# Hybrid GLA and SSD layer: the first head's k loaded and split in the start, half of q and k placed behind the last adaLN sums

## The chip, the cores and the metric

The kernel runs on one core of a Trainium2 chip. The metric is the device time of one execution in microseconds (us). Five engines work side by side, each on its own list of instructions in a fixed order: PE (matrix multiply), DVE (vector), ACT (scalar and copy), POOL (a second, slower vector engine) and SP (here it only issues DMAs).

## What is computed

One layer over 512 latent tokens and 256 context tokens of width 1024. A vector c gives six modulation parts (adaLN); the normed input, scaled and shifted by them, goes through one wide input projection, whose columns feed a gated linear attention branch (GLA, 4 heads, two directions) and a Mamba-2 branch (SSD, 4 groups, two directions). Both are merged under gates, projected and added; a SwiGLU feed-forward and a final norm follow. In short:

```python
ada = silu(c) @ w_ada + b_ada                  # sh1, sc1, g1, sh2, sc2, g2
h   = rms_norm(x, norm1_w) * (1 + sc1) + sh1   # latent; context with its own ada
q, k, v, r, lr_f, lr_b, z, xs, B, C, dt, ga, gb = split(h @ w_in)
g   = log_sigmoid(lr @ up + bias) / 16         # GLA gates of one direction
o_a = gla(q, k, v, g) both ways;  y_a = (rms_norm(o_a) * silu(r)) @ w_pa
o_b = ssd(xs, B, C, dt) both ways; y_b = rms_norm((o_b + d * xs) * silu(z)) @ w_pb
x   = x + g1 * ((sigmoid(ga) * y_a + sigmoid(gb) * y_b) @ w_out)
x   = x + g2 * swiglu(rms_norm(x, norm2_w) * (1 + sc2) + sh2)
out = rms_norm(x, final_norm_w)
```

## The kernel before, in words

Every matrix product is made in three passes, since its operands are split into a hi half of short mantissa and a lo half that holds the rest: hi x hH, hi x hL, lo x hH. A weight block of 512 KB is loaded by `load_raw` (L173, DMA on SP's queue, L176) into one of three buffers of the tag `raw`; `split_w` (L183) then makes hi by a copy on ACT (L188) and lo by a subtraction on DVE or, in some stages, POOL (L189). `load_w` (L194) gives both halves one of two buffers each (tags `whi`, `wlo`).

The start loads x, normalizes and transposes it (`xnT`), and makes the first adaLN parts in four batches: `ada_first` runs sixteen passes on PE over a batch of w_ada (L277, tile `ada`), copies the sum on ACT (`ar`, L280), turns it on PE (`adaT`, L283) and adds the bias on DVE (L288, then the scale `s`, L291). Each batch gives two of the eight k tiles of the modulated input: `h_of` makes hH on ACT (L299), the full value on DVE (L300) and hL on DVE (L301). The weights `misc` (the low-rank gate inputs and dt) and q of head 0 are loaded and split ahead in this block (the dictionary `ahead`).

`proj_cols` (L349) projects one block over the eight k tiles: `l_...` holds 512 latent columns (L361, L362, L366), `c_...` 256 context columns (L364, L365, L368), each in a PSUM bank of its own. `proj_rows` (L372) makes products by rows of tokens, `r_...`, for v, r and z (L386 to L388), its weights in two halves. Later adaLN columns are made one by one in `some_ada` (L329): every second call loads 512 KB (`raw_ada`) and sums it on POOL (L341, L343, L345), and a pass on PE finishes the one before (L336); the calls are spread over the projections, four of them in each v and r.

From misc's product come the GLA gates: copies into `M` (L396 to L398), their halves `MS` (L413 to L415), the matrix `U` (L407, L408), `pre` on PE (L470), three ACT functions and one DVE step (L472 to L475), then a write to memory, `gdr` (L476). The first GLA chain reads it back as `g` (L514) and makes sums with it on PE (`gc`, `kx`, `ky`, L501), which open the states `S`. At the end of the layer's first half the merge of both branches (`tgm`, `mt`, L967 to L978) runs beside the last block of w_pb and the start of w_out, which is scaled by g1 on POOL (L187); the scale of the second norm is made on DVE (`sc`, L952) with `n` (L950).

The order of the instructions on each engine is set by a scheduler that works on the whole program; `tc.high_priority()` and `tc.issue_after(instruction)` change the rank of what is written inside them.

## Time and profile before

| | us |
|---|---|
| median of 3 runs | 1431.89 (1430.45 to 1432.89) |
| profiled execution | 1434.66 |
| its span in the trace | 1432.9 |
| PE busy | 1357.3 (95%) |
| DVE busy | 871.0 (61%) |
| ACT busy | 502.2 (35%) |
| POOL busy | 465.4 (32%) |

The mean granted clock of TensorE in that execution is 0.981 of full speed. The profile's times count from the start of the span. A busy share is a mean over stages with different limits, so a stage is read from its own stretch of time: which engine stood still there, and what ended its wait.

### The profile page before, as it was taken

The numbers are of one execution on the slowest core, as the hardware profiler recorded it, in microseconds if no ns is written. First come the engines' busy times: TensorE is split into PE (matmuls) and PEld (weight loads), VectorE is DVE, ScalarE is ACT, GpSimd is POOL, SyncE is SP. The second block draws the span as 40 slices with busy tenths as digits, with TensorE's granted clock in tenths as the row PEclk, the third lists the DMA queues.
The fourth block names the chain that finished last, engine by engine and source line by source line (L and its number), as shares of the span: only waits on it lengthen the run. The fifth ranks groups of instructions, "written<-read, shape, count | busy, mean of one in ns | idle before, by whom it ended". The sixth has DMA issues, their size and how long they took to land.

```text
span 1432.9 us, 19032 instructions
## 1 busy us (share of the span) xinstructions
PE 1357.3 (95%) x7462; PEld 1152.4 (80%) x7462; DVE 871.0 (61%) x1292; ACT 502.2 (35%) x828; POOL 465.4 (32%) x333
## 2 busy tenths in 40 slices
PE   5999999999999999999899899999789999999997
PEld 3798999899888778877877787877578888888886
DVE  4559676563785787569758866766883343433225
ACT  6464333433444223433322342322243222222222
POOL 1355554245234433543253334113651122100001
PEclk9899999999999999999899999999999999999999
DMA  9363323334231343232322332557423333333331
GB/s 367 124 211 108 95 92 112 102 104 144 70 96 60 125 126 96 74 109 83 96 70 84 98 110 78 173 168 253 147 87 101 120 118 116 120 117 91 101 103 73
DMA packets 58010, 169.19 MB, mean 118 GB/s; under 512 B 6064, under 2 KB 10304, under 8 KB 57792
## 3 DMA queue, kind: packets, MB, share of 16 engines
q1 hardware_dynamic: 55328, 157.96, 34.0%
q0 software_dynamic: 2304, 9.64, 2.1%
q8 instruction: 59, 0.97, 0.3%
q10 hardware_dynamic: 288, 0.36, 0.1%
q14 instruction: 31, 0.25, 0.1%
HBM read 156.23 MB, written 11.72 MB: 117 GB/s over the span
## 4 chain that ended last, share of the span: by engine, by line
PE 66%; DVE 15%; DMA 9%; issue 6%; ACT 2%; POOL 2%; SPq 1%; POOLq 0%; DVEq 0%; ACTq 0%
DMA E<-cdr 5%; PE up L1056 3%; PE gate L1055 3%; PE gate L1056 3%; PE up L1055 3%; PE gate L1054 3%; PE up L1054 3%; PE db L204 3%; PE db L206 3%; PE db L205 3%; DVE E L747 2%; PE lv L501 2%; PE r_z L386 1%; PE pb_pb L632 1%; PE pb_pb L634 1%
## 5 line engine op out<-in xcount | busy, mean ns | idle before, releaser
L341 POOL TENSOR_TENSOR raw_ada<-raw_ada,cs 128x1024 f32<-128x1024 f32 x32 | 63.7, 1990 | 279.5 <-DMA raw_ada<-in_wts_dram 227.9
L747 DVE TENSOR_TENSOR E<-E,ebias 128x512 f32<-128x512 f32 x64 | 54.7, 859 | 49.4 <-DMA E<-cdr 49.3
L386 PE MATMUL r_z<-whi_z,hH 128*128 128x256 f32 x256 | 75.7, 298 | 6.6 <-DVE z L698 6.6
L343 POOL TENSOR_TENSOR raw_ada<-raw_ada 128x512 f32<-128x512 f32 x64 | 80.0, 1250 | 4.3
L388 PE MATMUL r_z<-whi_z,hL 128*128 128x256 f32 x256 | 76.9, 301 | 0.0
L387 PE MATMUL r_z<-wlo_z,hH 128*128 128x256 f32 x256 | 74.7, 293 | 0.0
L1054 PE MATMUL gate<-h2H,whi_gate 128*128 128x512 f32 (+1 forms) x192 | 71.8, 374 | 0.0
L1055 PE MATMUL gate<-h2L,whi_gate 128*128 128x512 f32 (+1 forms) x192 | 71.7, 373 | 0.0
L1056 PE MATMUL gate<-h2H,wlo_gate 128*128 128x512 f32 (+1 forms) x192 | 71.5, 373 | 0.0
L189 POOL TENSOR_TENSOR wlo_xs<-raw_xs,whi_xs 128x1024 fp32r<-128x1024 f32 x16 | 43.1, 2693 | 63.8 <-ACT whi_xs L188 63.8
L1056 PE MATMUL up<-h2H,wlo_up 128*128 128x512 f32 x160 | 63.0, 394 | 0.0
L1055 PE MATMUL up<-h2L,whi_up 128*128 128x512 f32 x160 | 62.3, 389 | 0.0
L1054 PE MATMUL up<-h2H,whi_up 128*128 128x512 f32 x160 | 62.2, 389 | 0.0
L189 DVE TENSOR_TENSOR wlo_gate<-raw_gate,whi_gate 128x1024 fp32r<-128x1024 f32 x20 | 33.2, 1661 | 45.2 <-ACT whi_gate L188 45.2
L189 DVE TENSOR_TENSOR wlo_down<-raw_down,whi_down 128x1024 fp32r<-128x1024 f32 x18 | 22.0, 1225 | 62.4 <-ACT whi_down L188 62.3
L386 PEld LDWEIGHTS r_z<-whi_z,hH 128*128 128x128 f32 x256 | 50.9, 200 | 9.2 <-DVE z L698 7.3
L170 POOL TENSOR_TENSOR rr_f<-rv_f,negh 128x1 f32<-128x1 f32 x4 | 2.6, 662 | 168.5 <-DVE rv_f L168 168.5
L189 POOL TENSOR_TENSOR wlo_z<-raw_z,whi_z 128x1024 fp32r<-128x1024 f32 x16 | 39.4, 2462 | 53.5 <-ACT whi_z L188 51.4
L386 PE MATMUL r_v<-whi_v,hH 128*128 128x256 f32 x192 | 55.7, 290 | 1.0 <-ACT whi_v L188 1.0
L205 PE MATMUL db<-wlo_down,fH 128*128 128x512 f32 x142 | 55.2, 389 | 0.0
L206 PE MATMUL db<-whi_down,fL 128*128 128x512 f32 x142 | 55.2, 389 | 0.0
L388 PE MATMUL r_v<-whi_v,hL 128*128 128x256 f32 x192 | 55.1, 287 | 0.0
(475 smaller groups left out, 4460.1 us busy)
## 6 DMA issues: line engine op xcount, KB each, us to landing
raw_ada<-in_wts_dram SPq DMA_DIRECT2D x32, 512.0 KB, 3.6
E<-cdr SPq DMA_DIRECT2D x64, 256.0 KB, 3.4
raw_gate<-in_wts_dram SPq DMA_DIRECT2D x22, 512.0 KB, 3.6
raw_up<-in_wts_dram SPq DMA_DIRECT2D x22, 512.0 KB, 3.5
raw_down<-in_wts_dram SPq DMA_DIRECT2D x22, 512.0 KB, 3.5
aw<-in_wts_dram SPq DMA_DIRECT2D x8, 1024.0 KB, 15.4
raw_xs<-in_wts_dram SPq DMA_DIRECT2D x16, 512.0 KB, 3.6
raw_z<-in_wts_dram SPq DMA_DIRECT2D x16, 512.0 KB, 3.7
```

The costliest lines, as they stand in the source:

```text
L189: (nc.gpsimd if split_pool[0] else nc.vector).tensor_tensor(lo, raw, hi.bitcast(F32), ALU.subtract)
L205: nc.tensor.matmul(out_, aH, bL, start=False, stop=False)
L206: nc.tensor.matmul(out_, aL, bH, start=False, stop=stop)
L341: nc.gpsimd.tensor_tensor(raw, raw, cs[:, :, 0:1].to_broadcast([P, KD, P]), ALU.mult)
L343: nc.gpsimd.tensor_tensor(raw[:, 0:n, :], raw[:, 0:n, :], raw[:, n:2 * n, :], ALU.add)
L386: nc.tensor.matmul(o, hH[:, kk, tk], hi[:, k, :], start=st, stop=False, skip_group_check=True)
L387: nc.tensor.matmul(o, hH[:, kk, tk], lo[:, k, :], start=False, stop=False, skip_group_check=True)
L388: nc.tensor.matmul(o, hL[:, kk, tk], hi[:, k, :], start=False, stop=sp, skip_group_check=True)
L747: nc.vector.tensor_tensor(ed, ed, ebias[:, d, n, hh].unsqueeze(2).to_broadcast([P, EH, P]), ALU.add)
L1054: nc.tensor.matmul(pts[kj][:, tk], hi[:, k, :], h2H[:, k, tk], start=(k == 0), stop=False)
L1055: nc.tensor.matmul(pts[kj][:, tk], hi[:, k, :], h2L[:, k, tk], start=False, stop=False)
L1056: nc.tensor.matmul(pts[kj][:, tk], lo[:, k, :], h2H[:, k, tk], start=False, stop=(k == KD - 1))
```

## The change

k of head 0 is loaded and split in the start block, right behind misc and q. Its halves, `k_hi` and `k_lo`, do not take the buffers of `whi` and `wlo` but two of the three `raw` buffers; they are created only when k's raw tile exists. The context product of k, c_k, takes the second half of the bank that holds c_misc, without a start flag of its own and ranked behind misc's first context matmul. The last four k tiles of q and of k in head 0 are ranked behind the last adaT matmul. The matmuls of the context products skip a check of the compiler on accumulation groups. v of head 0 no longer calls `some_ada`; the columns that it loaded move on to the calls behind it.

```diff
--- before.py
+++ after.py
@@ -183,6 +183,8 @@
     def split_w(key, hi, lo, row=None):
         with nullcontext() if in_start[0] else tc.high_priority():
             raw = load_raw(key)
+            if callable(hi):
+                hi, lo = hi(), lo()
             if row is not None:
                 nc.gpsimd.tensor_tensor(raw[:, 0, :], raw[:, 0, :], row, ALU.mult)
             nc.scalar.activation(hi, raw, AF.Copy)
@@ -267,7 +269,11 @@
         in_start[0] = True
         for key in (("misc",), ("q", 0)):
             ahead[key] = load_w(key)
+
+        ahead[("k", 0)] = split_w(("k", 0), *[lambda n=n: wp.tile([P, KD, P], F32R, tag="raw", name=f"k_{n}", bufs=3) for n in ("hi", "lo")])
         in_start[0] = False
+
+        ada_end = [None]
 
         def ada_first(b):
             pt = sm_bank(f"ada_{b}")
@@ -280,7 +286,7 @@
                 nc.scalar.activation(ar, pt, AF.Copy)
                 pt = sm_bank(f"adaT_{b}")
                 for j in range(4):
-                    nc.tensor.matmul(pt[:, 2 * j:2 * j + 2], ar[:, j * P:(j + 1) * P], sel, start=True, stop=True)
+                    ada_end[0] = nc.tensor.matmul(pt[:, 2 * j:2 * j + 2], ar[:, j * P:(j + 1) * P], sel, start=True, stop=True)
                 pv = pt[:, 0:8].rearrange("p (c j t) -> p c j t", c=2, t=2)
                 k0 = 2 * b
                 for c in range(2):
@@ -345,6 +351,8 @@
             nc.gpsimd.tensor_tensor(pr_, raw[:, 0, :], raw[:, 1, :], ALU.add)
             half_done.append((j, pr_))
 
+    early_cx, misc_start = [], []
+
 
     def proj_cols(key, with_ctx):
         if key[0] in ("q", "k") and key[1:2] != (0,):
@@ -355,17 +363,33 @@
         hi, lo = load_w(key)
         nm = "_".join(map(str, key))
         lat = mm_bank("l_" + nm)
-        cx = mm_bank("c_" + nm) if with_ctx else None
-        for k in range(KD):
-            st, sp = k == 0, k == KD - 1
-            nc.tensor.matmul(lat, hi[:, k, :], hH[:, k, 0:SEQ], start=st, stop=False)
-            nc.tensor.matmul(lat, hi[:, k, :], hL[:, k, 0:SEQ], start=False, stop=False)
-            if with_ctx:
-                nc.tensor.matmul(cx[:, 0:CTX], hi[:, k, :], hH[:, k, SEQ:NT], start=st, stop=False)
-                nc.tensor.matmul(cx[:, 0:CTX], hi[:, k, :], hL[:, k, SEQ:NT], start=False, stop=False)
-            nc.tensor.matmul(lat, lo[:, k, :], hH[:, k, 0:SEQ], start=False, stop=sp)
-            if with_ctx:
-                nc.tensor.matmul(cx[:, 0:CTX], lo[:, k, :], hH[:, k, SEQ:NT], start=False, stop=sp)
+
+        joined = key == ("k", 0)
+        if joined:
+            cx = early_cx[0][:, CTX:2 * CTX]
+        else:
+            cx = mm_bank("c_" + nm) if with_ctx else None
+        if key == ("misc",):
+            early_cx.append(cx)
+        first = key in (("q", 0), ("k", 0))
+        with ExitStack() as late_part:
+            for k in range(KD):
+                st, sp = k == 0, k == KD - 1
+                if joined and k == 0:
+                    late_part.enter_context(tc.issue_after(misc_start[0].ins))
+                if first and k == 4:
+                    late_part.enter_context(tc.issue_after(ada_end[0].ins))
+                nc.tensor.matmul(lat, hi[:, k, :], hH[:, k, 0:SEQ], start=st, stop=False)
+                nc.tensor.matmul(lat, hi[:, k, :], hL[:, k, 0:SEQ], start=False, stop=False)
+                if with_ctx:
+                    m_ = nc.tensor.matmul(cx[:, 0:CTX], hi[:, k, :], hH[:, k, SEQ:NT], start=st and not joined, stop=False,
+                                          skip_group_check=True)
+                    if key == ("misc",) and k == 0:
+                        misc_start.append(m_)
+                    nc.tensor.matmul(cx[:, 0:CTX], hi[:, k, :], hL[:, k, SEQ:NT], start=False, stop=False, skip_group_check=True)
+                nc.tensor.matmul(lat, lo[:, k, :], hH[:, k, 0:SEQ], start=False, stop=sp)
+                if with_ctx:
+                    nc.tensor.matmul(cx[:, 0:CTX], lo[:, k, :], hH[:, k, SEQ:NT], start=False, stop=sp, skip_group_check=True)
         return lat, cx
 
 
@@ -373,7 +397,7 @@
         banks = [mm_bank(f"r_{'_'.join(map(str, keyf(0)))}_{b}") for b in range(ntile // 2)]
         for kh in range(2):
             hi, lo = load_w(keyf(kh))
-            if keyf(0)[0] in "vr":
+            if keyf(0)[0] in "vr" and keyf(0)[:2] != ("v", 0):
                 some_ada()
                 some_ada()
             for i in range(ntile):
```

What the scheduler makes of it shows in the order of the instructions. First PE around the fourth adaT (`adaT`, fed by `sel` and `ar`), before and then changed:

```order
L361 MATMUL l_q_583<-hH,whi_q_149 128x512
L362 MATMUL l_q_583<-hL,whi_q_149 128x512
L366 MATMUL l_q_583<-hH,wlo_q_150 128x512
L283 MATMUL adaT_373<-sel,ar_371 128x2 x4
L361 MATMUL l_misc<-hH,whi_misc 128x512
L361 MATMUL l_q_583<-hH,whi_q_149 128x512
L364 MATMUL c_misc<-hH,whi_misc 128x256
L362 MATMUL l_misc<-hL,whi_misc 128x512
L365 MATMUL c_misc<-hL,whi_misc 128x256
L366 MATMUL l_misc<-hH,wlo_misc 128x512
L368 MATMUL c_misc<-hH,wlo_misc 128x256
L361 MATMUL l_misc<-hH,whi_misc 128x512
```

```order
L382 MATMUL l_k_617<-hH,k_hi 128x512
L383 MATMUL l_k_617<-hL,k_hi 128x512
L390 MATMUL l_k_617<-hH,k_lo 128x512
L289 MATMUL adaT_379<-sel,ar_377 128x2 x4
L382 MATMUL l_q_589<-hH,whi_q_149 128x512
L383 MATMUL l_q_589<-hL,whi_q_149 128x512
L390 MATMUL l_q_589<-hH,wlo_q_150 128x512
L382 MATMUL l_q_589<-hH,whi_q_149 128x512
L383 MATMUL l_q_589<-hL,whi_q_149 128x512
L390 MATMUL l_q_589<-hH,wlo_q_150 128x512
L382 MATMUL l_k_617<-hH,k_hi 128x512
L383 MATMUL l_k_617<-hL,k_hi 128x512
```

Before, six tiles of q stand ahead of adaT and misc directly behind it; now it is four tiles of q and four of k, and behind adaT come two more of each before misc. The first r_v follows 36 rows behind adaT, and c_k (named c_misc<-hH,k_hi) 31 rows of r_v later.

Second, DVE from misc's copies to the products of the gates, before and then changed:

```order
L396 COPY M<-l_misc 16x512
L396 COPY M<-c_misc 16x256
L189 TENSOR_TENSOR wlo_k_612<-raw_k_613,whi_k_611 128x1024
L413 CAST MS_462<-M 32x768
L408 TENSOR_TENSOR U<-early_in,U 32x1024
L415 TENSOR_TENSOR MS_462<-M,MS_462 32x768
L189 TENSOR_TENSOR wlo_v_0_683<-raw_v_0_684,whi_v_0_682 128x1024
L398 COPY M<-l_misc 64x512
L398 COPY M<-c_misc 64x256
L413 CAST MS_466<-M 32x768
L415 TENSOR_TENSOR MS_466<-M,MS_466 32x768
```

```order
L420 COPY M<-l_misc 16x512
L420 COPY M<-c_misc 16x256
L191 TENSOR_TENSOR wlo_v_0_682<-raw_v_0_683,whi_v_0_681 128x1024
L437 CAST MS_468<-M 32x768
L422 COPY M<-l_misc 64x512
L422 COPY M<-c_misc 64x256
L437 CAST MS_472<-M 32x768
L439 TENSOR_TENSOR MS_468<-M,MS_468 32x768
L439 TENSOR_TENSOR MS_472<-M,MS_472 32x768
L432 TENSOR_TENSOR U<-early_in,U 32x1024
L191 TENSOR_TENSOR wlo_v_1_760<-raw_v_1_761,whi_v_1_759 128x1024
L461 COPY kv_616<-c_misc 128x256
```

Before, k's lo half stands behind the first copies, and v's first between the two MS products; now v's first half stands where k's was, all copies come ahead of the MS products, U goes last, and the copy of c_k (kv<-c_misc) follows v's second half.

Third, PE where the second direction of head 0's gates is first read (`gc_1`), before and then changed:

```order
L361 MATMUL l_q_1301<-hH,whi_q_1295 128x512
L362 MATMUL l_q_1301<-hL,whi_q_1295 128x512
L366 MATMUL l_q_1301<-hH,wlo_q_1296 128x512
L501 MATMUL gc_1_1021<-mkr,g_1_1019 128x128 x2
L501 MATMUL kx_1_1028<-g_1_1019,mkr 128x384
L501 MATMUL gc_1_1021<-mkr,g_1_1019 128x128
L501 MATMUL ky_1_1030<-g_1_1019,mkr 128x256
L501 MATMUL gc_1_1021<-mkr,g_1_1019 128x128
L501 MATMUL ky_1_1030<-g_1_1019,mkr 128x128
L501 MATMUL S_0_0_1051<-kv_610,kd_0_1014 128x256 x2
L361 MATMUL l_q_1301<-hH,whi_q_1295 128x512
```

```order
L390 MATMUL l_q_1280<-hH,wlo_q_1275 128x512
L342 MATMUL ada_1308<-one,apr_1272 128x1
L382 MATMUL l_k_1324<-hH,whi_k_1318 128x512
L383 MATMUL l_k_1324<-hL,whi_k_1318 128x512
L390 MATMUL l_k_1324<-hH,wlo_k_1319 128x512
L382 MATMUL l_k_1324<-hH,whi_k_1318 128x512
L383 MATMUL l_k_1324<-hL,whi_k_1318 128x512
L390 MATMUL l_k_1324<-hH,wlo_k_1319 128x512
L385 MATMUL c_k_1325<-hH,whi_k_1318 128x256
L389 MATMUL c_k_1325<-hL,whi_k_1318 128x256
L525 MATMUL gc_1_1000<-mkr,g_1_998 128x128 x2
L525 MATMUL kx_1_1007<-g_1_998,mkr 128x384
```

Before, nine matmuls of head 1's q stand ahead of gc_1 and 15 behind S_0_0; now all 24 stand ahead of it, with six of head 1's k and two of its context product.

## Rows read from the trace of the kernel before

**Rows 1.** The page: busy time and share of the span, instructions by engine.
```profile
PE 1357.3 (95%) x7462; PEld 1152.4 (80%) x7462; DVE 871.0 (61%) x1292; ACT 502.2 (35%) x828; POOL 465.4 (32%) x333
```

**Rows 2.** Stretches: from:to, length, busy (count) per engine, PEclk, DMA share, GB/s.
```profile
51.00:54.30 3.30, 0.92 (x4) 0.53 (x4) 2.35 (x7) 2.50 (x4) 0.00 (x0) 1.00 0.00 0
54.30:57.70 3.40, 3.40 (x10) 2.83 (x11) 2.34 (x4) 0.00 (x0) 1.05 (x2) 0.50 0.02 5
57.70:61.00 3.30, 2.38 (x11) 1.38 (x10) 2.54 (x4) 1.28 (x2) 0.65 (x2) 1.00 0.80 202
109.60:116.00 6.40, 6.35 (x20) 5.20 (x21) 5.61 (x9) 5.67 (x8) 5.49 (x5) 0.52 0.28 90
116.00:150.00 34.00, 32.74 (x224) 29.98 (x222) 33.09 (x54) 13.68 (x23) 18.05 (x13) 1.00 0.27 90
```

**Rows 3.** PE in order of time: start, us, line, operation, out<-in, count [idle <-releaser].
```profile
41.35 0.40 PE L361 MATMUL l_q<-hH,whi_q 128*128 128x512 f32 x1
...
42.49 1.06 PE L277 MATMUL ada<-aw,csw 128*32 128x512 f32 x8
...
50.01 0.95 PE L283 MATMUL adaT<-sel,ar 128*128 128x2 f32 x8
52.32 0.50 PE L361 MATMUL l_misc<-hH,whi_misc 128*128 128x512 f32 x1 [1.37 <-ACT hH L299]
...
54.26 0.79 PE L362 MATMUL l_misc<-hL,whi_misc 128*128 128x512 f32 x1 [1.06 <-DVE hL L301]
...
58.26 0.28 PE L368 MATMUL c_misc<-hH,wlo_misc 128*128 128x256 f32 x1
...
59.39 0.50 PE L361 MATMUL l_k<-hH,whi_k 128*128 128x512 f32 x1 [0.39 <-ACT whi_k L188]
...
60.65 0.50 PE L366 MATMUL l_k<-hH,wlo_k 128*128 128x512 f32 x1 [0.53 <-DVE wlo_k L189]
...
65.77 0.28 PE L364 MATMUL c_k<-hH,whi_k 128*128 128x256 f32 x1
...
66.60 1.09 PE L470 MATMUL pre<-U,MS 96*128 96x512 f32 x4
...
69.57 0.28 PE L386 MATMUL r_v<-whi_v,hH 128*128 128x256 f32 x1
```

**Rows 4.** ACT in order of time, 30 to 73 us.
```profile
37.01 2.51 ACT L299 ACTIVATE hH<-xnT,ada,s 128x512 fp32r<-128x512 f32 x4 [2.62 <-DVE s L291]
...
58.27 1.06 ACT L188 ACTIVATE whi_k<-raw_k 128x1024 fp32r<-128x1024 f32 x1 [4.32 <-issue]
...
67.03 2.07 ACT L472 ACTIVATE ge<-pre 128x512 f32<-128x512 f32 x4 [0.24 <-PE pre L470]
```

**Rows 5.** DVE in order of time, 30 to 76 us.
```profile
51.00 0.23 DVE L288 TENSOR_TENSOR ada<-adaT,vecs 128x4 f32<-128x4 f32 x2 [9.46 <-PE adaT L283]
...
59.39 1.20 DVE L189 TENSOR_TENSOR wlo_k<-raw_k,whi_k 128x1024 fp32r<-128x1024 f32 x1
...
66.68 0.42 DVE L398 COPY M<-c_misc 64x256 f32<-64x256 f32 x1
```

**Rows 6.** PE in order of time, 105 to 117 us.
```profile
109.65 1.19 PE L501 MATMUL gc<-mkr,g 128*128 128x128 f32 x4 [2.83 <-DMA g<-gdr]
...
115.40 0.75 PE L361 MATMUL l_q<-hH,whi_q 128*128 128x512 f32 x1
```

**Rows 7.** The page: costliest groups, the two POOL lines of an adaLN sum.
```profile
L341 POOL TENSOR_TENSOR raw_ada<-raw_ada,cs 128x1024 f32<-128x1024 f32 x32 | 63.7, 1990 | 279.5 <-DMA raw_ada<-in_wts_dram 227.9
...
L343 POOL TENSOR_TENSOR raw_ada<-raw_ada 128x512 f32<-128x512 f32 x64 | 80.0, 1250 | 4.3
```

**Rows 8.** Stretch from 845 to 895 us, columns as in rows 2.
```profile
845.00:895.00 50.00, 50.00 (x256) 40.88 (x256) 30.59 (x48) 17.23 (x29) 20.90 (x12) 0.95 0.26 85
```

**Rows 9.** DVE in order of time, around the merge: scale of the second norm.
```profile
993.02 2.40 DVE L952 SCALAR_TENSOR_TENSOR sc<-sc,n 128x512 f32<-128x512 f32 x1 [2.61 <-DMA n<-in_rows_dram]
```

**Rows 10.** PE's waits from 970 to 1062 us: total, times, longest.
```profile
PE ob L205 <- DVE wlo_out L189: 5.9, 3, 3.0
```

## The prediction

> **What bounds the kernel now.** First the page's busy times: PE works 1357.3 of 1432.9 us, 95% [rows 1]. The change takes no matmul away, so it can only shorten stretches in which PE stands still or runs at the lower clock. Next the table by stretch, for the place that the change touches [rows 2]: from 51.0 to 54.3 us PE is busy 0.92 of 3.30; from 54.3 to 57.7 it is busy all the time, but with a granted clock of 0.50, which is the 1.2 GHz level; from 57.7 to 61.0 it is busy 2.38 of 3.30. That is 2.38 + 0.92 us of idleness and 1.70 us (half of 3.40) of lower clock: 5.0 us lost in ten. Then PE's own instructions say why [rows 3]. The fourth adaT runs at 50.01, and the rest of misc waits for what follows from it: 1.37 us for hH, 1.06 us for hL. Behind misc come q's last two tiles, and then k waits 0.39 us for the hi and 0.53 us for the lo half of its weights. PE has nothing else to do: of q six tiles were already used up ahead of adaT, and k's split on ACT starts only at 58.27 [rows 4]. On DVE the 9.46 us ahead of 51.00 are idle time that ends with the same adaT [rows 5].
>
> **The change, part by part.** *k split early.* Two more instructions enter the start: k_hi on ACT, 1.06 us by whi_k's row, in an idle stretch of 2.62 us ahead of the third hH batch [rows 4]; and k_lo on DVE, 1.20 us by wlo_k's row [rows 5], ahead of the third batch's ada and s, which come 1.2 us later. That batch is needed by the misc tiles after 41 us, and DVE has 9.46 us free behind it, so I cost both at nothing; without that cover it would be 1.2 us. The same two instructions leave the place at 58.27 and 59.39. k's load itself is no new DMA: it is third among the weights on SP in both kernels.
>
> *The list on PE.* I count what lies between the first l_q at 41.35 and the first r_v at 69.57 [rows 3]. 22 matmuls of 512 columns fill 60.65 to 65.77, 0.233 each; 24 of 256 columns and four pre of 512 fill 65.77 to 69.57, which leaves 0.12 for one of 256. The list is 24 l_q, 24 l_k and 12 l_misc (60 x 0.233 = 14.0), 12 c_misc and 24 c_k (36 x 0.12 = 4.3), sixteen ada passes (2 x 1.06), adaT (0.95) and four pre (0.93): 22.3 us. The stretch took 28.22, so 5.9 us went into waits, the lower clock and the starts behind waits, 5.0 of them as read above. In the new order four tiles of q and four of k run ahead of adaT, and twelve matmuls of 0.233, 2.8 us, behind it. The first hL that PE now needs comes 3.3 us after adaT's end (54.26 against 50.96); ahead of it stand those 2.8 us and 0.8 us of hH matmuls, so the latency is covered by 0.3 us. Without c_k and pre, which now stand behind v's first matmuls, r_v could start at 41.35 + 22.3 - 2.9 - 0.9 = 59.8. What is late next: v. Its hi half takes misc's buffer, so it can start only when misc's last hi pass is through; after that PE has five matmuls, some 1.2 us, and the split needs 1.06 on ACT and then 1.20 on DVE behind the first copies into M. By the same kind of wait at k (0.39 + 0.53 = 0.92) I take 1.1 us for v, bounds 0.5 and 2.3, and 0.4 us (0 to 1) where pre now stands, ahead of which the c_k pass is done and little is left to hide M, MS and U. So this stretch gives 5.9 - 1.5 = 4.4 us.
>
> *The gates.* Their first matmul stood 8.34 us behind misc's last (66.60 against 58.26) [rows 3]. Five matmuls (1.05 us) ahead of r_v's 59.8 misc ends at about 58.8 now, 0.5 later; one split instead of two lies inside that chain (-1.2), but U has gone last in it (its own length is bounded by the splits', 0 to 1.2), and ACT makes v's second hi half (1.06) ahead of the first gate instead of behind it. I take the gates 1.4 us later, bounds 0 and 3. This is what counts next: at 109.65 PE stands 2.83 us for g of the second direction [rows 6], which comes out of those gates, and the wait costs a second time: from 109.6 to 116.0 the granted clock is 0.52. Before, 15 l_q came behind that block (from 115.40 on); now they stand ahead of it, with 6 l_k and 2 c_k: 21 x 0.233 + 2 x 0.12 = 5.1 us. PE comes 4.4 us earlier and does 5.1 us more, so it arrives about 0.7 us later than it did and still waits. With g later by 1.4 us, equal work is done 5.1 - 1.4 = 3.7 us earlier: the term is -0.7 against the stretch ahead of it. Head 1's k stands ahead of the gates' last two writes on SP, so its weights need not be late for this.
>
> *The adaLN sums.* Two loads of 512 KB and their sums leave v of head 0; each later pair slides up, and two come to lie in the gate and SSD stage near 845 to 895 us. A sum is 1.99 us and twice 1.25 us on POOL [rows 7] and one small addition: about 4.5, 9 for both. POOL is busy 20.90 of those 50 us, and PE waits for nothing there: 50.00 of 50.00 [rows 8]. Cost taken: 0.
>
> *The merge.* With other instructions in other places the order near 970 to 1015 us changes too: DVE's scale of the second norm, which waits 2.61 us for n [rows 9] and stood behind the last block's weights, goes ahead of two of them; the loads of g1 and of that norm go ahead of the four hres loads. Upwards I bound this with that 2.61, downwards with half of the 5.9 us that PE waits for the output weights [rows 10], since they come through g1. Nothing in the trace says which is nearer; I take 0.
>
> **Sum.** -4.4 + 0.7 + 0 + 0 = -3.7 us. The profiled execution took 1434.66 us and would take 1431.0. The median of the runs shown is 2.77 us below that execution, so I forecast **1428.2 us**.
>
> **Rivals.** *The second direction's gates set the end* (13%). DVE is busy 33.09 of the 34.0 us from 116 to 150 [rows 2], and it works on what g brings. If this chain, not PE's list, ends that stretch, all that was won waits there, and the gates' delay of 0 to 1.4 us shows: 1431.9 to 1433.3. For it: PE and DVE are both near full (32.74 against 33.09). Against it: PE's matmuls of head 1 can fill.
>
> *c_k waits for the copies of M* (5%). c_k now writes the second half of the bank that holds c_misc, and c_misc's last copy into M ended at 67.10 [rows 5]. By the list r_v starts at 59.8 + 1.1, and c_k stands 31 of its matmuls (3.7 us) behind, at 64.6. If the copies kept their time, PE would stand 2.5 us there: -3.7 + 2.5 = -1.2, 1430.7 us. Against it: in the new order the copies stand ahead of the products MS that came first before. The Trainium skill speaks for the wait: PSUM — Partial Sum Buffer, section PSUM bank collisions raise a hardware error, says that two engines must not use one bank on the same partitions at once and that access is to be guarded by bank, whichever columns are meant; no row of this trace shows it, since each product had a bank of its own.
>
> *The merge gives back its 2.61 us* (5%): -1.1, 1430.8.
>
> *The change doesn't do what it says* (3%): the new cover behind adaT is too short or v's weights take over k's wait in full, the lower clock comes back, and 1431.9 stays.
>
> *Slower: POOL in the SSD stage* (8%). The two moved sums stand among POOL's steps of the state (S_b, S_f) and of the norm (rr_y) of the last group. If each sum delays a step that PE waits for, both cost 9 us: -3.7 + 9 = +5.3, 1437.2. It decides from 6.6 us of such waits on (3.7 won and 2.9 over). Against it: POOL's 29 idle us there, and a PE without a wait [rows 8].
>
> **How the numbers follow.** The forecast with its own bounds holds 66%. A measurement of this kernel tells some 0.2%, 2.9 us, from no change. Faster by more than that is the forecast alone: 0.66. The four cases between 1430.7 and 1433.3 are no change: 0.26. The SSD case is slower: 0.08. The low end takes the gates not later at all (-5.1) and the merge better by 3.0: 1431.9 - 8.1 = 1423.8. The high end is the first rival's, 1433.3; only the slower case and the far corners lie outside.
>
> **What would show it.** Right: twelve l_k matmuls ahead of the fourth adaT; no stretch at a granted clock of 0.50 between 51 and 61 us; the first r_v near 61 with a wait of about 1 us for whi_v and wlo_v; pre near 68; gc of the second direction near 111 behind 24 l_q; PE still without waits near 845 to 895. Wrong: a wait for hL or k_lo ahead of 61, c_k behind a DVE copy, PE idle between 116 and 150 for DVE, or new waits for y or pb weights late.

## The result, and the profile after

The changed kernel takes 1436.66 us (median of 9 runs, 1434.28 to 1441.27), the kernel before 1431.89 beside it (9 runs, 1427.28 to 1433.46): ratio 1.0054, 95% interval 1.0039 to 1.0070. It is 4.8 us slower and lies above the range given; that it would be slower at all had been given a chance of 0.08.

First PE's start in order of time, to be held against [rows 3]:

```profile
50.77 0.39 PE L382 MATMUL l_k<-hH,k_hi 128*128 128x512 f32 x1
...
51.45 0.95 PE L289 MATMUL adaT<-sel,ar 128*128 128x2 f32 x8
52.26 0.48 PE L382 MATMUL l_q<-hH,whi_q 128*128 128x512 f32 x1
...
60.49 0.38 PE L410 MATMUL r_v<-whi_v,hH 128*128 128x256 f32 x1 [0.34 <-ACT qT L454]
61.32 0.39 PE L411 MATMUL r_v<-wlo_v,hH 128*128 128x256 f32 x1 [0.45 <-DVE wlo_v L191]
...
65.01 0.28 PE L385 MATMUL c_misc<-hH,k_hi 128*128 128x256 f32 x1
...
108.81 0.61 PE L525 MATMUL gc<-mkr,g 128*128 128x128 f32 x4
```

This is as forecast: k ahead of adaT, no wait behind it, r_v at 60.49 instead of 69.57 with two waits of 0.8 us together (the first ends with ACT's qT, not with whi_v as forecast: whi_v was done by 59.95), c_k (the row c_misc<-hH,k_hi) without a wait. The table by stretch answers to [rows 2] and [rows 8]:

```profile
51.00:54.30 3.30, 3.30 (x20) 2.87 (x19) 0.94 (x5) 1.40 (x3) 0.00 (x0) 1.00 0.03 7
54.30:57.70 3.40, 3.40 (x19) 2.85 (x18) 3.11 (x7) 1.11 (x2) 0.00 (x0) 1.00 0.00 0
57.70:61.00 3.30, 2.83 (x13) 1.89 (x11) 2.52 (x4) 2.08 (x3) 1.68 (x3) 1.00 0.49 130
105.00:116.00 11.00, 8.48 (x47) 6.80 (x46) 10.38 (x16) 6.29 (x10) 7.26 (x7) 1.00 0.55 188
116.00:150.00 34.00, 29.43 (x223) 27.90 (x222) 32.61 (x57) 11.76 (x21) 12.54 (x9) 1.00 0.27 89
845.00:895.00 50.00, 49.87 (x261) 40.94 (x261) 30.67 (x44) 16.11 (x27) 28.73 (x18) 0.97 0.25 85
```

The stretch at 1.2 GHz is gone (clock 1.00 from 51 to 61 us), and most of the idle time with it (0.47 us are left). But from 116 to 150 us PE is busy 29.43 us instead of 32.74, and DVE 32.61 of 34.

Where the lead went shows when the same matmul is looked up in several profiles: the first of v (head 0), the first l_k of head 3 (the last head), the last z product of the SSD stage, the first with the output weights (ob), the first transpose of the feed-forward's input (hT) and the first of the feed-forward's second half (db). The kernel before was profiled twice more (look1, look2), the changed one once more (again); the last three rows are runs explained below. Start in us:

```
               r_v     l_k, head 3   last r_z   ob        hT        db
before         69.57     299.14       860.93    994.96   1050.09   1304.99
look1          68.87     297.70       856.08    990.12   1046.52   1300.62
look2          69.75     298.26       856.62    990.68   1044.41   1299.13
after          60.49     295.80       860.96   1000.66   1050.56   1306.82
again          60.45     299.37       860.80   1000.16   1049.99   1306.03
b_light        69.66     291.71       851.92    985.99   1040.41   1294.22
light          60.54     287.27       851.22    992.34   1042.01   1298.96
light_v3       60.28     287.43       847.32    981.38   1033.05   1286.96
```

By the means of the rows (three of before, two of the change) the change is 8.9 us ahead at r_v, 0.8 at head 3's k, 3.0 behind at the end of the SSD stage, and 4.8 behind at db. So three things have to be explained: some 3 of the 3.7 us forecast are missing by head 3; the SSD stage takes 3.8 us more; what follows takes 1.8 more. (One profile of a kernel is not enough here: the three of before differ by 4.8 us at the last r_z, and at head 3's k after is 2.6 us ahead of their mean, again 1.0 behind it.)

What PE lost on the way to head 3 can be estimated from the tables by stretch: its idle time, plus the share of the stretch that the granted clock lacked to full speed. In us:

```
               51-61   61-105   105-150   150-200   200-250
before           5.0      0.0       7.5       1.4       0.0
look1            5.1      0.0       7.5       0.0       0.0
look2            6.0      0.0       7.0       0.5       0.0
after            0.5      0.3       7.1       0.5       1.0
again            0.5      0.3       9.7       0.0       3.3
b_light          5.9      1.7       0.1       0.0       0.0
light            0.4      0.4       2.2       0.0       0.0
gates_first      0.0      5.7       6.1       0.0       0.0
```

The 4.9 us won from 51 to 61 us are real. From 105 to 150 us the kernel before lost 7.0 to 7.5 us as well, part of it at the lower clock, so the stretch from 116 to 150 us in one profile of each overstates the difference: the change lost about as much there in after and 2.4 more in again, and from 200 to 250 us another 1.0 and 3.3 where before lost nothing. There PE waits for ek, which DVE makes (again, 200 to 250 us: total, times, longest):

```profile
PE lv L525 <- DVE ek L608: 3.1, 2, 1.7
```

### The profile page after: what moved, and what is told of

Same layout as the page of the kernel before. It is cut to its first block, busy times and chain, and to the rows that moved or that the text cites. A ratio compares the mean times of both kernels' runs of the same rounds, so it can differ in the third digit from the quotient of the medians.

```text
span 1434.7 us, 19029 instructions
## 1 busy us (share of the span) xinstructions
PE 1355.6 (94%) x7462; PEld 1150.1 (80%) x7462; DVE 877.0 (61%) x1292; ACT 502.6 (35%) x828; POOL 471.5 (33%) x333
## 4 chain that ended last, share of the span: by engine, by line
PE 64%; DVE 17%; DMA 8%; issue 6%; ACT 2%; POOL 2%; SPq 0%; POOLq 0%; DVEq 0%; ACTq 0%
DMA E<-cdr 5%; PE up L1080 3%; PE gate L1079 3%; PE gate L1078 3%; PE gate L1080 3%; PE up L1079 3%; PE up L1078 3%; PE db L206 3%; PE db L207 3%; PE db L208 3%; DVE E L771 2%; PE pb_pb L658 1%; PE pb_pb L656 1%; PE pb_pb L657 1%; PE lv L525 1%
## 5 line engine op out<-in xcount | busy, mean ns | idle before, releaser
L771 DVE TENSOR_TENSOR E<-E,ebias 128x512 f32<-128x512 f32 x64 | 58.7, 923 | 53.4 <-DMA E<-cdr 53.4
L349 POOL TENSOR_TENSOR raw_ada<-raw_ada 128x512 f32<-128x512 f32 (+1 forms) x64 | 80.8, 1265 | 3.9
L411 PE MATMUL r_v<-wlo_v,hH 128*128 128x256 f32 x192 | 55.3, 288 | 0.4 <-DVE wlo_v L191 0.4
## 6 DMA issues: line engine op xcount, KB each, us to landing
E<-cdr SPq DMA_DIRECT2D x64, 256.0 KB, 3.5
```

What stands on the lines that cost most here:

```text
L349: nc.gpsimd.tensor_tensor(raw[:, 0:n, :], raw[:, 0:n, :], raw[:, n:2 * n, :], ALU.add)
L411: nc.tensor.matmul(o, hH[:, kk, tk], lo[:, k, :], start=False, stop=False, skip_group_check=True)
L771: nc.vector.tensor_tensor(ed, ed, ebias[:, d, n, hh].unsqueeze(2).to_broadcast([P, EH, P]), ALU.add)
```

## The experiments

Each ratio is to the kernel before, run on the same chip beside it.

**One part at a time.** again is the changed kernel once more. only_sums is the kernel before in which v of head 0 makes no adaLN call; keep_sums is the changed kernel in which it makes them; in r_takes the changed kernel's r of head 0 makes them, so that the order behind 845 us is that of before.

The edit of only_sums (keep_sums makes the reverse one in the changed kernel), and that of r_takes:

```diff
-            if keyf(0)[0] in "vr":
+            if keyf(0)[0] in "vr" and keyf(0)[:2] != ("v", 0):
```

```diff
-                some_ada()
-                some_ada()
+                for _ in range(4 if keyf(0)[:2] == ("r", 0) else 2):
+                    some_ada()
```

> The changed kernel once more, for a second profile. Both theories: again 0.3 to 0.7% over the kernel before. The profile on record loses about 6 us against before between 545 and 930 us, though from 250 to 845 us the order of the instructions is the same on every engine. If this loss has a fixed cause there, the second profile loses at the same places by the same 5 to 6 us; if it is an accident of how DVE and POOL steps meet, the places and the amount differ by several us.

> The kernel before with one part of the change alone: v of head 0 doesn't load adaLN columns, so two sums move to the gates near 845 to 895 us; the order from 845 us on becomes that of the changed kernel, the start stays as it was. Theory late (the moved sums and the merge behind them cost the time): 4 to 6 us over before. Theory SSD (the lead won in the start is lost between 545 and 850 us): within 2 us of before.

> The changed kernel with one part undone: v of head 0 loads its adaLN columns as before, so from head 1 on the order is that of the kernel before. Theory late: most of the start's 3 to 4 us are kept, 1428 to 1430 us where before has 1432. Theory SSD: no gain or a loss, 1432 to 1437. In the start these loads now share one free raw buffer with v's and r's weights, which may cost up to 2 us there.

> The changed kernel, but r of head 0 takes the four calls that v gave up, so that from head 1 on the adaLN sums and the order are those of the kernel before. Theory late: 3 to 4 us under before, about 1428. Theory SSD: at or over before, 1432 to 1437.

Measured: again 1437.08 (1.0040, 1.0025 to 1.0055), only_sums 1437.0 (1.0045, 1.0028 to 1.0062), keep_sums 1438.33 (1.0059, 1.0040 to 1.0079), r_takes 1434.38 (1.0023, 1.0009 to 1.0036). The moved sums alone cost as much as the whole change (1437.0 against 1430.57 beside it, 6.4 us); the new start alone, with the sums left where they were, costs no less. So it is no simple sum of a good start and bad sums. keep_sums and r_takes don't show the start by itself either: with the calls in head 0 PE stands idle for 5.5 and 4.4 us from 61 to 105 us, where after has 0.3 (keep_sums for dt_v and wlo_v, r_takes for a sum and wlo_q).

**Is it the gates' own lateness?** gates_first is r_takes with q from tile 3 on and all of k behind the fourth adaT, and k from tile 2 on behind misc's last matmul, so that the gates get the lead; b_q3 is the kernel before with q from tile 3 on behind adaT and nothing else.

The edit of gates_first to r_takes, and of b_q3 to the kernel before:

```diff
-                if first and k == 4:
+                if first and k == (3 if key[0] == "q" else 0):
                     late_part.enter_context(tc.issue_after(ada_end[0].ins))
+                if joined and k == 2:
+                    late_part.enter_context(tc.issue_after(misc_end[0].ins))
```

```diff
+            if key == ("q", 0) and k == 3:
+                late_part.enter_context(tc.issue_after(ada_end[0].ins))
```

> The kernel before, once more, for a second profile. The profiled execution shown of it took 1434.66 us, 3 to 4 us more than its median; this one should be nearer 1430.5 us and show where a usual execution is shorter, by stretch.

> The kernel before, a third profile: as the last, 1427 to 1434 us. The start up to 100 us is the same within 0.3 us in all of them; what differs lies behind.

> The changed kernel with the adaLN calls in r of head 0 as in the run r_takes, and the first matmuls in another order: the fourth adaT right behind its sum (q from tile 3 and k wholly behind it), and k from tile 2 on behind misc's last matmul, so that misc ends about 3 us earlier than in the changed kernel. From head 1 on the order is that of the kernel before. Theory gates (the lead of the start is lost because head 0's gate chain is not earlier): pre moves from 68.7 to about 64.5 us, gc of the second direction and the end of head 0's chain come 3 to 5 us earlier than before, and the time is 1425 to 1429 us. Theory SSD (whatever lead is lost between 425 and 930 us): the lead is there at 320 us, but the time is 1431 to 1436 us.

> The kernel before with one rank alone: q of head 0 from tile 3 on is queued behind the fourth adaT, which then runs about 2 us earlier, with 9 matmuls (2.1 us) behind it instead of none; k, its weights and the adaLN calls stay as they were. Theory gates: misc, pre and head 0's chain come about 2 us earlier, and the time is 1427 to 1429.5 us. Theory SSD: 1430 to 1434 us.

Measured: the two looks 1430.29 and 1428.84; gates_first 1431.02 (0.9995, 0.9974 to 1.0017), b_q3 1431.42 (1.0005, 0.9987 to 1.0023). The loss goes, but no gain appears, although r_v starts at 60.01 and 66.04 in them. In gates_first pre moved to 64.4 as forecast, and gc of the second direction to 105.83, 3.2 us ahead of before's mean. But PE, which got there earlier still, now waits 5.17 us for g instead of the 2.83 of [rows 6]:

```profile
105.83 1.19 PE L529 MATMUL gc<-mkr,g 128*128 128x128 f32 x4 [5.17 <-DMA g<-gdr]
```

So there the wait for the gates takes most of the lead; at head 3's k 1.4 us of it are left (297.0 against 298.4).

**POOL.** What else can take it shows in DVE's instructions in order of time, after the change, from 109 to 126 us:

```profile
109.39 1.18 DVE L856 COPY dtb<-early_in 128x128 f32<-128x128 f32 x1
...
111.71 2.05 DVE L863 COPY_PREDICATED early_in<-early_in,dt_v 128x384 f32<-128x384 int32 x1 [0.59 <-ACT early_in L860]
113.65 1.61 DVE L867 SCALAR_TENSOR_TENSOR early_in<-early_in 128x384 f32<-128x384 f32 x1
...
120.92 0.68 DVE L601 TENSOR_TENSOR eq<-eq,qT 128x512 f32<-128x512 f32 x1
121.53 0.47 DVE L580 SCALAR_TENSOR_TENSOR S<-S,gtot,S 128x256 f32<-128x256 f32 x1
121.92 2.00 DVE L601 TENSOR_TENSOR eq<-eq,qT 128x512 f32<-128x512 f32 x1
123.84 1.76 DVE L608 TENSOR_TENSOR ek<-ek,kv 128x512 f32<-128x512 f32 x1
```

and POOL's of the same kernel and time:

```profile
108.17 2.31 POOL L482 TENSOR_TENSOR rw<-rw,rsm 128x512 f32<-128x512 f32 x1 [3.15 <-DVE rw L481]
...
111.39 1.91 POOL L347 TENSOR_TENSOR raw_ada<-raw_ada,cs 128x1024 f32<-128x1024 f32 x1 [0.49 <-issue]
113.38 1.46 POOL L349 TENSOR_TENSOR raw_ada<-raw_ada 128x512 f32<-128x512 f32 x1
...
121.28 2.09 POOL L347 TENSOR_TENSOR raw_ada<-raw_ada,cs 128x1024 f32<-128x1024 f32 x1 [4.86 <-DMA raw_ada<-in_wts_dram]
123.45 2.73 POOL L349 TENSOR_TENSOR raw_ada<-raw_ada 128x512 f32<-128x512 f32 x2
```

The same eq takes 0.68 us at 120.92 and 2.00 at 121.92: the second began while POOL's product (from 121.28, 2.09 us) was running, and ended some 0.5 us behind its end; ek then began within POOL's addition and took 1.76. In the kernel before the same chain has these rows:

```profile
116.26 0.22 DVE L832 COPY dtb<-early_in 128x128 f32<-128x128 f32 x1
...
118.01 0.16 DVE L542 COPY gtot<-qd 128x4 f32<-128x4 f32 x1
118.08 0.42 DVE L533 TENSOR_TENSOR kd<-kd,kv 128x256 f32<-128x256 f32 x1
118.41 1.88 DVE L542 COPY gtot<-qd 128x4 f32<-128x4 f32 x1
...
120.82 0.60 DVE L839 COPY_PREDICATED early_in<-early_in,dt_v 128x384 f32<-128x384 int32 x1
121.31 0.54 DVE L843 SCALAR_TENSOR_TENSOR early_in<-early_in 128x384 f32<-128x384 f32 x1
```

Here dtb, copy_predicated and the step behind it are short (0.22, 0.60, 0.54 against 1.18, 2.05, 1.61), and another instruction is hit: a copy of four columns takes 1.88 us, having begun 0.03 us behind this one of POOL's (the same kernel):

```profile
118.38 1.90 POOL L341 TENSOR_TENSOR raw_ada<-raw_ada,cs 128x1024 f32<-128x1024 f32 x1 [2.12 <-DMA raw_ada<-in_wts_dram]
```

Which DVE instruction meets POOL's sums is a matter of phase. The Trainium skill (SBUF — State Buffer, Who interferes with whom) has the rule: DVE and GpSimd (POOL) share one pair of ports as an exclusive lock, a DVE instruction with two SBUF inputs (against a POOL instruction that reads SBUF) or in a 2-port mode contends for it, and issue order decides who waits for the whole of the other's instruction. The trace agrees, with 2.00 against 0.68 us.

Hold-up, in the following, is the sum over the DVE instructions that start in a stretch of what each took beyond the shortest time of the same instruction (same tiles and shape, same place in their order) in any profile, where that is over 0.4 us. From 110 to 320 us it is 21.0, 21.7 and 21.4 us in the three profiles of before, 30.0 and 29.4 in the two of the change (of it 9.7, 9.6, 8.8 against 12.0, 13.0 up to 160 us). only_sums (30.5), keep_sums (29.6) and r_takes (28.8) are like the change, gates_first (20.6) and b_q3 (22.9) like before: the same two groups as in the ratios. To test it, light and b_light take most of the POOL work out of the first 20 sums (the result of those columns is left incomplete: the product with c and two of three additions), and later and b_later keep all work but make no adaLN call in head 0 and in q, k and v of head 1.

The edit of light and b_light, and that of later and b_later:

```diff
-            nc.gpsimd.tensor_tensor(raw, raw, cs[:, :, 0:1].to_broadcast([P, KD, P]), ALU.mult)
-            for n in (4, 2):
+            if j >= 36:
+                nc.gpsimd.tensor_tensor(raw, raw, cs[:, :, 0:1].to_broadcast([P, KD, P]), ALU.mult)
+                for n in (4, 2):
```

```diff
-        if key[0] in ("q", "k") and key[1:2] != (0,):
+        if key[0] in ("q", "k") and key[1] > 1:
...
+                for _ in range({("r", 1): 4, ("v", 2): 3, ("r", 2): 3, ("v", 3): 4, ("r", 3): 4}.get(keyf(0)[:2], 0)):
+                    some_ada()
```

> The changed kernel, in which the first 20 adaLN sums after the start (all that run before 345 us) leave out the product with c and two of the three additions: POOL works 0.5 us on each instead of 5, the loads stay. Seen so far: DVE instructions that start just behind the start of such a POOL instruction take 1.2 to 2.3 us instead of 0.4 to 0.7; summed over 110 to 160 us that is 8.8 to 9.7 us in the three profiles of the kernel before and 13.3 in the changed one, and 11.2 to 11.7 against 17.3 from 160 to 320 us. Theory 'POOL holds DVE up': with the sums gone the start's lead comes through; r_v number 145 and the work at 320 us stand 3 to 4 us earlier here than in b_light. Rival 'gates': the chain of the gates itself is late (adaT 1.4, pre 2.1 us later); then light stands no earlier than b_light at these places, within 1 us. Time: 1425 to 1431 by the first, 1428 to 1434 by the second, since the loss in the SSD stage and at the merge (2 to 5 us) stays in both.

> The kernel before with the same 20 sums cut to 0.5 us. Both theories: the 9 us by which DVE was held up from 110 to 160 us go, most of them beside PE's work; the time falls by 0 to 4 us, 1427 to 1431. It is the partner of light: what counts is where equal work stands in the two at 135, 160 and 320 us (3 to 4 us earlier in light by 'POOL holds DVE up', equal within 1 us by 'gates').

> The changed kernel with all its work, but with no adaLN call in head 0 nor in q, k and v of head 1; r of head 1 and v and r of heads 2 and 3 make more of them (44 calls in the projections of the heads, as before the change), so that the first sums on POOL run behind the DVE-bound stretch of 105 to 150 us, where PE is full. 'POOL holds DVE up': head 0's chain (dg, S, o) comes 3 us or more earlier than in the changed kernel, the time is 1425 to 1431. 'Gates': no gain at 135 us, 1433 to 1438. It could also move the hold-up to 200 to 340 us, where the sums now stand closer: PE would then wait for DVE there, which no kernel but those without sums in v of head 0 showed so far.

> The kernel before with the same places of the adaLN calls as in later. 'POOL holds DVE up': 0 to 3 us below before (1427 to 1431), and later 3 us below it. 'Gates': equal to before or a little below, and later not below it.

Measured: light 1428.05 (0.9977, 0.9962 to 0.9991), b_light 1424.38 (0.9950, 0.9931 to 0.9968). b_light's time lies below its range, light's in both of its ranges, so the places have to decide. The hold-up from 110 to 320 us falls to 0.6 and 3.0 us, and at l_k of head 3 light stands 4.44 us ahead of b_light (287.27 against 291.71). The stretches (from:to, length, busy per engine in the order PE, PEld, DVE, ACT, POOL, clock) of the change and of light:

```profile
105.00:150.00 45.00, 37.91 (x267) 34.70 (x266) 42.99 (x72) 18.05 (x30) 19.81 (x15) 1.00 0.34 113
150.00:320.00 170.00, 168.39 (x1082) 152.42 (x1081) 113.32 (x187) 64.24 (x124) 77.06 (x60) 1.00 0.30 99
```

```profile
105.00:150.00 45.00, 42.85 (x316) 40.55 (x315) 35.47 (x72) 20.17 (x32) 5.03 (x6) 1.00 0.35 115
150.00:320.00 170.00, 170.00 (x1109) 155.32 (x1108) 94.14 (x190) 66.03 (x128) 20.46 (x23) 1.00 0.33 103
```

With POOL out of the way DVE does the same chain in 35 of 45 us instead of 43, PE works 5 us more in them, and the start's lead, 4.4 us as forecast, arrives (light_v3, below, has the same: 287.43). So the first of the three losses needs POOL's sums; that is shown, by one profile of b_light and two with the new start. Not shown is that the 9 us of longer hold-up are what does it, and not the 21 us that before has too: without the sums PE is full from 116 to 320 us in both kernels of the pair, and then any lead of its list comes through. The ends, however, are not ordered that way: light is 3.7 us slower than b_light.

later and b_later missed every range given: 1449.02 (1.0132, 1.0108 to 1.0157) and 1445.97 (1.0099, 1.0075 to 1.0123). The sums now stand too close; PE waits in its own order for POOL's result (later, 200 to 430 us: total, times, longest):

```profile
PE ada L342 <- POOL apr L351: 8.7, 4, 3.7
```

**The late order.** light_v3 and v3_takes are light and the changed kernel in which v of head 3 makes four adaLN calls more, so that the order behind 845 us is that of before. b_piece and piece_v3 (before, and v3_takes) cut each sum into seven short POOL instructions.

The edit of the calls, and that of the sums:

```diff
+                for _ in range(4 if keyf(0)[:2] == ("v", 3) else 2):
+                    some_ada()
```

```diff
+            for k in range(0, KD, 2):
+                nc.gpsimd.tensor_tensor(raw[:, k:k + 2, :], raw[:, k:k + 2, :], cs[:, k:k + 2, 0:1].to_broadcast([P, 2, P]), ALU.mult)
+            for k in (0, 2):
+                nc.gpsimd.tensor_tensor(raw[:, k:k + 2, :], raw[:, k:k + 2, :], raw[:, k + 4:k + 6, :], ALU.add)
+            nc.gpsimd.tensor_tensor(raw[:, 0:2, :], raw[:, 0:2, :], raw[:, 2:4, :], ALU.add)
```

> light (the changed kernel with the first 20 sums cut to 0.5 us) in which v of head 3 makes four adaLN calls more, so that no pair is left for the stretch behind 845 us and the order of the work there is that of the kernel before. In light, from 930 us to the end equal work lost 4.9 us against the kernel before, in b_light 0.2; in after and again 3.0 and 2.7. Theory 'merge': this loss hangs on the late order (pb waits 2.6 us for wlo_pb, behind the scale of the second norm); then the time is 2.5 to 4 us below light's, 1424 to 1426. Rival 'stages come out even': what is won ahead is lost behind it, whatever the order; then it is light's 1428. The loss of 5 us that light shows against 2 in b_light from 425 to 930 us should stay by both, if it is due to the start; if it goes too, it came from the late order as well (1421 to 1423).

> The changed kernel with four adaLN calls more in v of head 3, all its work done: the start as in the change, head 0 and 1 as in the change, behind 845 us the order of before. By 'merge' 2.5 us below the changed kernel's 0.5% above before, so 0.3% above before, 1433 to 1435; by the rival no difference to it.

> The kernel before with each adaLN sum cut into seven short POOL instructions (four products of 256 elements, three additions of 256, the last of 128) instead of four of up to 1024. 'POOL holds DVE up' says that a DVE instruction that starts behind a POOL one waits for that instruction's end: with 0.4 to 0.6 us a piece instead of 1.9 and 1.3 a hit costs 0.5 us at most; held-up time from 110 to 320 us falls from 21 us to under 10, and the time by 1 to 5 us (b_light, without the sums, gained 6.3). If each piece holds DVE anew, the sum of the hits stays and the time does not fall.

> v3_takes with the same cut of the sums. If hold-up and merge are what took the lead of the start, this has the lead (4 us at 320 us against b_piece), the late order of before, and is the fastest kernel with all its work: 1424 to 1430, at or below b_piece; what the SSD stage takes back (3 us) is the uncertain part.

Measured: light_v3 1419.62 (0.9911, 0.9882 to 0.9939), v3_takes 1434.49 (1.0026, 1.0005 to 1.0047), b_piece 1434.99 (1.0030, 1.0011 to 1.0048), piece_v3 1431.18 (1.0007, 0.9987 to 1.0026). light_v3's ratio is 0.39% (5.6 us) below b_light's, each against before on its own chip, with intervals that overlap by 0.1%; in the profiles it stands 4.3 us ahead at head 3, 4.6 at the last r_z and 7.3 at db. So without POOL's sums, and with the late order of before, the start's lead lasts; the 2.7 us behind the last r_z, where the order of the two is the same, are not the start's. By the ratios light_v3 lies 0.66% below light, and its time is below even the lowest of the three ranges expected (1421 to 1423); v3_takes lies in the range of 'merge'. The forecast looked for the late loss at the merge. DVE of the changed kernel there, in order of time:

```profile
986.46 0.69 DVE L976 SCALAR_TENSOR_TENSOR sc<-sc,n 128x512 f32<-128x512 f32 x1 [5.77 <-DMA n<-in_rows_dram]
987.67 1.22 DVE L191 TENSOR_TENSOR wlo_pb<-raw_pb,whi_pb 128x1024 fp32r<-128x1024 f32 x1
```

and PE's waits from 930 to 1060 us, of the kernel before, of the changed kernel and of light_v3:

```profile
PE ob L205 <- DVE wlo_out L189: 5.9, 3, 3.0
PE hT L1022 <- DVE hn L1019: 5.3, 1, 5.3
```

```profile
PE ob L207 <- DVE wlo_out L191: 5.8, 3, 2.6
PE pb_pb L658 <- DVE wlo_pb L191: 2.6, 1, 2.6
PE hT L1046 <- DVE hn L1043: 2.3, 2, 1.2
PE up L1078 <- DVE rv_h L168: 1.5, 1, 1.5
```

```profile
PE hT L1047 <- DVE hn L1044: 4.6, 1, 4.6
PE ob L207 <- DVE wlo_out L191: 2.6, 3, 1.1
```

The scale of the second norm, now ahead of the last w_pb blocks on DVE, waits 5.77 us for n, and PE 2.63 behind it for wlo_pb ([rows 9] had 2.61 for n, behind those blocks). From the last r_z to the first db the four profiles with the new late order take 445.2 to 447.7 us (after 445.86, again 445.23, light 447.74, only_sums 446.14), the three of before 442.5 to 444.5, light_v3 439.6 and v3_takes 440.2: about 2 us or more go here.

The wait at the merge is not what is left of it, though. The changed kernel comes to the first ob 5 to 6 us later (139.7 and 139.4 us behind the last r_z, before 134.0, 134.0 and 134.1), but from there to the first hT it needs 49.9 and 49.8 us instead of 55.1, 56.4 and 53.7, with less of a wait for hn. At hT the two are even: 189.6 and 189.2 us behind the last r_z against 189.2, 190.4 and 187.8. What stays lies behind hT: from the first hT to db the four profiles with the new late order take 256.0 to 256.9 us, and all others here 253.6 to 255.3. That is 1.6 us by the means, and PE's wait of 1.5 us for rv_h, a step of the second norm on DVE, stands there (also in again, only_sums and light; in the three of before it is 0.5 us at most). Nor is all of light_v3's lead over light the late order's: 3.9 of the 12.0 us at db are there at the last r_z, and 5.1 come from there to hT, where kernels with one and the same order differ by 4.7 us (light_v3 185.7, look1 190.4).

v3_takes lost 2.4 us to PE's wait for a sum (as in later) near 315 us, where its extra calls stand. b_piece missed: cutting the sums brought the hold-up from 110 to 320 us down from 21 to 16 us but made the kernel slower, so the sum of the hold-up alone does not order the times. piece_v3 missed its range of 1424 to 1430; against v3_takes it went the expected way, by 0.2%, with intervals that overlap.

**All the work, and faster?** piece_ga makes the four calls at the first early ga and gb tiles instead, with the short pieces; act_ga has the same places, and the product with c on ACT.

The edit of the calls in both, and that of the product in act_ga:

```diff
         if key[0] in ("ga", "gb"):
-            some_ada()
+            for _ in range(3 if key[1] == 0 else 1):
+                some_ada()
```

```diff
+            for k in range(KD):
+                nc.scalar.activation(raw[:, k, :], raw[:, k, :], AF.Copy, scale=cs[:, k, 0:1])
```

> The changed kernel with all its work; the four calls that v of head 0 gave up are made by the first early ga and gb tiles (near 245 us, where POOL has no sum), and each sum is cut into seven short POOL instructions as in piece_v3. piece_v3 stood 3.0 us ahead of the kernel before at 301 us and lost 5.8 us at 302 to 319 us, where its four extra calls made PE wait; without that loss, and with the late order of before, the theories 'POOL holds DVE up' and 'merge' give 3 to 5 us below piece_v3: 1426 to 1428. If stages only come out even, it is 1431 as piece_v3.

> The same places of the calls; the product with c of each sum is made on ACT (eight activations of 128 elements with a scale by partition) and only the three additions on POOL (1.3, 0.7 and 0.5 us). 'POOL holds DVE up' gives about half of the hold-up from 110 to 320 us (30 us in the changed kernel) and 1425 to 1430. Against it: ACT is busy 17 to 18 of 20 us from 70 to 90 us, and the eight activations of the first sum stand ahead of the gates there; if they cost the gates 2 us, as much is lost at 135 us and the time is 1431 to 1435.

Measured: piece_ga 1431.58 (1.0008, 0.9992 to 1.0024), act_ga 1438.31 (1.0043, 1.0025 to 1.0060). Both missed their ranges; piece_ga ends where before does. act_ga cut the hold-up from 110 to 320 us to 17 us, but its first gc starts at 110.5 us (after: 97.1). The likely reason is ACT, whose eight products of a sum take 0.40 us each, 2.5 us together (32.7 us for the 13 sums from 60 to 200 us); no run tests it by itself:

```profile
L348 ACT ACTIVATE raw_ada<-raw_ada,cs 128x128 f32<-128x128 f32 x104 | 32.7, 395 | 19.3 <-DMA raw_ada<-in_wts_dram 19.3
```

No version with all its work was faster than the kernel before.

**Left open: the SSD stage.** From l_k of head 3 to the last r_z the change takes 565.2 and 561.4 us, before 561.8, 558.4 and 558.4, though from some 355 to 865 us the order of the instructions is the same on every engine. (The expectation of again says from 250 us; up to some 350 us it still differs.) PE's waits from 425 to 845 us, of look2 and of the change:

```profile
PE yT L501 <- DVE y L783: 6.8, 5, 2.9
PE r_z L386 <- DVE z L698: 6.4, 3, 3.2
```

```profile
PE yT L525 <- DVE y L807: 11.5, 6, 3.5
...
PE r_z L410 <- DVE z L722: 1.7, 2, 0.9
```

The waits for y, which DVE makes while POOL splits weights, are longer, those for z shorter. From l_k of head 3 to the last r_z the waits for y add up to 11.5 and 11.8 us in the change and 6.4, 9.2 and 6.8 in before, those for z to 4.1 and 4.8 against 6.6, 4.7 and 6.4. Single DVE steps are held up by 2.2 us there in both kernels, partly others in each profile.

The place is nearly the same each time: from the 384th to the 576th r_z, about 590 to 721 us, after takes 137.1 us, again 134.9, only_sums 135.0 and light 134.6, the three of before 132.7, 131.2 and 131.7, light_v3 130.2 and keep_sums 131.6. So the new start is not what is needed for this loss: only_sums has it with the old start (its profile is of its slowest execution, 1443.81 us), and light_v3 and keep_sums have the new start without it. It goes with the moved sums, though they lie outside this stretch; but b_q3 (134.4) and r_takes (134.0) come near without them. What makes it was not settled.

## Why the prediction was wrong

- *k split early, the list on PE:* right. r_v starts at 60.49 (forecast 60.9), its two waits are 0.8 us (1.1 taken), no half clock, c_k without a wait. The rival on the copies of M falls, because the copies came early: the last ended at 62.80 (before: 67.10), and c_k started at 65.01. So no row here shows the wait that guarding by bank, the rule of the Trainium skill (PSUM — Partial Sum Buffer, PSUM bank collisions raise a hardware error), could have made.
- *The adaLN sums, "Cost taken: 0":* the step that failed most. With this part of the change alone, only_sums takes 6.4 us more than the kernel before (ratio 1.0045). The sums were priced by POOL's own busy time (9 us beside 29 idle us near 845 to 895 us), not by what they do to DVE where they start, nor by what the new places do to the order behind. That stretch itself did stay full (49.87 of 50.00), so the slower rival, as written, did not happen: that the measured time lies near its 1437.2 is luck.
- *The gates:* the lateness was about as taken (pre at 68.73 against 66.60, 2.1 us; 1.4 taken, bounds 0 and 3), and gc of the second direction starts at 108.81 (again 110.79), without a wait for g in the row; forecast was near 111. Up to there "equal work is done 5.1 - 1.4 = 3.7 us earlier" held. What failed is the step from there to the end of the kernel, that such a lead stays: the work that PE did ahead was filler (head 1's products), and PE then lacks it: by the means of the table above it loses 1.1 us more than before from 105 to 150 us, and 2.2 us, waiting for DVE, from 200 to 250 us, where before loses nothing. The rival that the second direction's gates set the end had this mechanism, a chain on DVE and not PE's list, at 13%; "PE's matmuls of head 1 can fill" was the wrong ground against it. Against b_light the gates of light are as late (pre at 68.8 and 66.7), and yet the lead arrives; so lateness alone does not take it, and POOL's sums have to be there. Hold-up on DVE from 110 to 320 us is 8.3 us more in the change than in before's three profiles (29.7 against 21.4 by the means). gates_first, where PE waits 5.17 us for g, shows that the gates can take a lead too.
- *The merge, 0 between bounds of +2.61 and -3.0:* the wait that gives the upper bound did come, 2.63 us on PE, but it is won back by hT. What the late order costs, 1.6 us, lies behind hT, a place that the prediction did not name; that 1.8 us at db look like this bound is luck.
- *The sum:* -0.8 instead of -3.7 at head 3, +3.8 in the SSD stage (cause open; it goes with the moved sums), +1.8 behind it: +4.8 by the profiles, +4.8 by the medians. That light_v3 stands 4.3 us ahead of b_light at head 3 and 4.6 at the last r_z shows the -4.4 of the start to be right where POOL's sums are gone.

## What to carry to other kernels

Before filling a wait on the busiest engine with work from later, look at the stretch that loses this work: if another engine's chain sets its end, the wait only moves there. Where DVE and POOL work side by side, price a POOL instruction by its length on DVE's chain as well, and look in the trace for DVE instructions that take far longer than the same ones elsewhere. A scheduler's order far behind an edit can take part of what the edit gives: compare the late order too, put it back for a test, and follow equal work past the wait that you suspect, since a wait there may be won back a little later.

## What was not expected of the hardware

A copy of four columns took 1.88 us instead of 0.16, a copy_predicated of 384 elements 2.05 instead of 0.60, and the tensor_scalar that makes early_in of 384 elements 1.33 instead of 0.35, each while POOL instructions of 1.6 to 1.9 us ran. Eight activations of 128 elements with a scale by partition took 2.5 us together (0.395 each, overlapping), longer than POOL's one product (1.9).
